# 64, 128 and 32 bytes of gap between the SBUF pools of a two-layer decoder trunk

## The chip, the cores and the metric

The kernel runs on one core of a Trainium2 chip, as one launch. The metric is the device time of that launch in microseconds (us); several runs are taken, and their median counts. The change moves data within SBUF, the core's on-chip memory: 128 partitions, in each of which a tile occupies one range of byte addresses.

## The reference

The program is a decoder trunk of two layers over a sequence of T = 1024 tokens with D = 1024 features, all in float32.

```python
for i in range(2):
    shift_t, scale_t, gate_t, shift_c, scale_c, gate_c = split(silu(c) @ ada_w[i] + ada_b[i], 6)
    h = rmsnorm(x, norm_g[i, 0]) * (1 + scale_t) + shift_t
    y = gla_mixer(h) if i == 0 else diff_mixer(h)
    x = x + gate_t * y
    h = rmsnorm(x, norm_g[i, 1]) * (1 + scale_c) + shift_c
    y = square(relu(h @ mlp_w1[i])) @ mlp_w2[i]          # 1024 -> 4096 -> 1024
    x = x + gate_c * y
return rmsnorm(x, final_g)
```

`gla_mixer` is gated linear attention with 4 heads (keys of 128, values of 256 features), `diff_mixer` differential softmax attention with 8 heads. Both begin with a projection of `h` and end with one of their output (`w_o`).

## The kernel before, in words

**Numbers in two parts.** TensorE gets every large product as three matmuls. `split` (L111) writes a float32 tile as a rounded part (`hi`, by ScalarE) and a remainder (`lo`, by VectorE, here DVE); `mm3` (L115) multiplies hi by hi, hi by lo and lo by hi into one accumulator. So the lines L116, L117 and L118 are the three matmuls of every product, and each group of the profile with these lines stands three times. A matmul has a loaded operand (`lhsT`, 128 x 128, brought into the array by a weight load that the profile shows as PEld) and a streaming one (`rhs`, up to 512 columns). The weight load for the next matmul runs while the present one streams.

**The stages.** Layer 0: the prologue, the GLA projections and their chunked recurrence (`pv`, `pq`, `pk`, then `pr` for the output gate), then `stretch` (L724): output projection, norm, MLP. Layer 1: the attention with its projections `pp` woven between scores and values by a schedule written out by hand, then `stretch` again, and the final norm. The MLP goes through 8 chunks of 512 inner features: for each, 2 halves of 512 tokens times 4 tiles of inner activations `hd` (8 products over `h` each), then 2 halves times 8 output tiles (4 products over `hd` each), which makes 192 matmuls over `h` and 192 over `hd`. In the last chunk the second half of the tokens is taken in two slices of 256 columns. Products go to the accumulators `acc`, `pr`, `pq`, `pk`, `pp`, `pv`; the residual add (L712, DVE) empties the MLP's second product.

**Which operand is which.** In `acc`, `pr`, `pq` and `pk` the weight (`whi`, `wlo`) is loaded and `h` or `hd` streams. In `pp` and `pv` it is the other way round: `h_hi`, `h_lo` are loaded, and `whi`, `wlo` stream, 384 or 256 columns wide (272 in head 0, where 16 more columns of the weight come along).

**Where the tiles lie.** SBUF pools are stacked in the order in which they are opened, and each buffer is rounded up to 32 bytes a partition. `const` comes first, then `wsp` (L89: 5 buffers each of `whi` and `wlo`, 4352 bytes = 17 x 256), `wraw` (L90: 2 x 4352), and `hp` (L91: `h`, 32 buffers of 2048). All three sizes are multiples of 256, so `h` and the weights begin at the same place modulo 256, and as the matmuls take slices at multiples of 512 bytes, each pair of operands does too. The one exception is GLA's head 0: its value weights are `[P, 4, 272]`, whose rows are 1088 = 4 x 256 + 64 bytes apart, so that successive `k` of four begin at 0, 64, 128 and 192 modulo 256 above the weights' base.

In `stretch` four pools follow: `sm` (small columns), `tp` (5 x 2048), `xp` (the residual `x`, tiles of 2048) and `hid` (`hd`, 16 x 2048). Layer 0 opens them in the order sm, tp, xp, hid (L726). `sm` has three small tiles of two buffers there, 6 x 32 = 192 bytes, so `hd` lies 192 bytes above the weights modulo 256. Layer 1 opens xp, hid, tp, sm (L727), and `hd` lies at 0. Two pools of layer 1's attention (`dx`, and `xa1` for half of `x`) are allocated from the other end of SBUF.

Of the kernel before, what the change touches and what calls it, by code (L numbers as in the profile page):

```python
# [10 lines left out]
F32 = mybir.dt.float32  # L11
# [10 lines left out]
P = 128  # L22
# [60 lines left out]
def trunk(ctx: ExitStack, tc, a, out):  # L83
    nc = tc.nc
    pe, act, dve, pool = nc.tensor, nc.scalar, nc.vector, nc.gpsimd
# [2 lines left out]
    const = ctx.enter_context(tc.tile_pool(name="const", bufs=1))  # L88
    wsp = ctx.enter_context(tc.tile_pool(name="wsp", bufs=5))  # L89
    wraw = ctx.enter_context(tc.tile_pool(name="wraw", bufs=2))  # L90
    hp = ctx.enter_context(tc.tile_pool(name="hp", bufs=2 * KT))  # L91
    dram = ctx.enter_context(tc.tile_pool(name="dram", bufs=1, space=DRAM))
    mm = ctx.enter_context(tc.tile_pool(name="mm", bufs=2, space=PSUM))
# [41 lines left out]
    def wcols(w, c0, n, pinned=False):  # L135

        return weight(w.rearrange("(k p) n -> p k n", p=P)[:, :, c0:c0 + n], [P, KT, n], pinned)
# [5 lines left out]
    def new_half():  # L143
        return [(hp.tile([P, HT], F32R, name="h_hi", tag="hhi"), hp.tile([P, HT], F32R, name="h_lo", tag="hlo"))
                for _ in range(KT)]
# [80 lines left out]
    def gscale(l, j):  # L226

        sc = mod[:, l, (3 * j + 1) * KT:(3 * j + 2) * KT]
        i = NG_ROW + (2 * l + j) * KT
        dve.scalar_tensor_tensor(out=gs[:, 2 * l + j, :], in0=sc, scalar=1.0, in1=colsT[:, i:i + KT],  # L230
                                 op0=ALU.add, op1=ALU.mult)

    def mcols(l, i):
        return mod[:, l, i * KT:(i + 1) * KT]
# [445 lines left out]
    def out_proj(h, half, w_o, acc, done, ahead=False, ready=None):  # L680


        rows, ends = KT - 1 if ahead else KT, []
        ws = [wcols(w_o, n * P, P) for n in range(4)]
        if ahead:
            yield
        for n0 in (0, 4):
            now, ws = ws, []
            for n in range(4):
                pt = acc()  # L690
                for k in range(rows):
                    mm3(pt, now[n][0][:, k, :], now[n][1][:, k, :], *h[k][half], k == 0, k == rows - 1)
                    if k == rows - 1:
                        ends.append((n0 + n, half, pt))
                    while ends and (ready is None or ready()):
                        i = done(*ends.pop(0))
                        if n0 == 0:
                            with tc.issue_after(i.ins):
                                ws.append(wcols(w_o, (4 + len(ws)) * P, P))
                    yield  # L700
        if ahead:
            w = weight(w_o.rearrange("(k p) n -> p k n", p=P)[:, rows:, :], [P, 1, D])
            for n in range(KT):
                pt = acc()
                mm3(pt, w[0][:, 0, n * P:(n + 1) * P], w[1][:, 0, n * P:(n + 1) * P], *h[rows][half], True, True)
                done(n, half, pt)
                yield

    def residual(l, x):
        def add(kt, half, psum, cols=slice(0, HT), gate=2):  # L710
            t = x[kt][half][:, cols]
            return dve.scalar_tensor_tensor(out=t, in0=psum, scalar=mcols(l, gate)[:, kt:kt + 1], in1=t, op0=ALU.mult,  # L712
                                            op1=ALU.add)
        return add

    def load_x(x, xp, halves, queue=nc.sync):
        for half in reversed(halves):
            for k in range(KT):
                x[k][half] = xp.tile([P, HT], F32, name=f"x{k}_{half}")
        for half in halves:  # L720
            for k in range(KT):
                queue.dma_start(out=x[k][half], in_=xs[k, :, half * HT:(half + 1) * HT])

    def stretch(l, h, w_o, ada_todo, after, x=None):  # L724
        with ExitStack() as g:
            order = (("sm", 2), ("tp", 5), ("xp", 1), ("hid", 4))  # L726
            order = order if l == 0 else (order[2], order[3], order[1], order[0])  # L727
            pools = {n: g.enter_context(tc.tile_pool(name=n, bufs=b, reuse_waits="tile")) for n, b in order}
            sm, tp, xp, hid = (pools[n] for n in ("sm", "tp", "xp", "hid"))
            ps = g.enter_context(tc.tile_pool(name="lp", bufs=1, space=PSUM, reuse_waits="tile"))  # L730
            ps2 = g.enter_context(tc.tile_pool(name="lp2", bufs=4, space=PSUM, reuse_waits="tile"))
            ga = g.enter_context(tc.tile_pool(name="ga2", bufs=2, reuse_waits="tile")) if ada_todo else None
            turn = [0]

            def acc_tile():
                turn[0] += 1
                shared = turn[0] % 3 == 0
                return (mm if shared else ps2).tile([P, HT], F32, name="acc", tag="mm" if shared else "mx")

            started = x is not None  # L740
            x = x or [[None, None] for _ in range(KT)]
            gscale(l, 1)
            load_x(x, xp, [half for half in range(2) if x[0][half] is None], nc.sync)
            add = residual(l, x)
            h2 = [[None, None] for _ in range(KT)]
            for half in range(2):
                if half or not started:
                    for _ in out_proj(h, half, w_o, acc_tile if half else acc_mm, add):
                        pass
                for k, t in enumerate(new_half()):  # L750
                    h2[k][half] = t
                norm_mod(x, half, h2, gs[:, 2 * l + 1, :], mcols(l, 3), tp, sm, ps)
            h = h2

            w1, w2 = a["mlp_w1"][l], a["mlp_w2"][l]
            sums = []
            for c in range(FF // 512):
                ws = [wcols(w1, c * 512 + n * P, P) for n in range(4)]
                hd = [[None, None] for _ in range(4)]
                for half in range(2):  # L760
                    for n in range(4):
                        pt = acc_tile()
                        for k in range(KT):
                            pe_last = mm3(pt, ws[n][0][:, k, :], ws[n][1][:, k, :], *h[k][half], k == 0, k == KT - 1)
                        if half and n < len(sums):
                            with tc.issue_after(pe_last.ins):
                                ada_sums(*sums[n], ps)
                        r = tp.tile([P, HT], F32, name="relu", tag="t")
                        act.activation(out=r, in_=pt, func=AF.Relu)  # L769
                        dve.tensor_tensor(out=r, in0=r, in1=r, op=ALU.mult)  # L770
                        hd[n][half] = [hid.tile([P, HT], F32R, name="hd", tag=f"hd{half}{i}") for i in range(2)]
                        split(hd[n][half][0], hd[n][half][1], r)
                ws = [weight(w2.rearrange("(f p) n -> p f n", p=P)[:, 4 * c:4 * c + 4, n * 256:(n + 1) * 256],
                             [P, 4, 256]) for n in range(4)]
                last = c == FF // 512 - 1
                for half, cols in ((0, slice(0, HT)), (1, slice(0, 256)), (1, slice(256, HT))) if last else \
                        ((0, slice(0, HT)), (1, slice(0, HT))):
                    w = cols.stop - cols.start
                    finish = after(half, cols, x, tp, sm, ps, acc_tile) if last else None
                    for n in range(KT):  # L780
                        pt = acc_tile()[:, :w]
                        wh, wl = ws[n // 2]
                        c0 = (n % 2) * P
                        for f in range(4):
                            mm3(pt, wh[:, f, c0:c0 + P], wl[:, f, c0:c0 + P], *(t[:, cols] for t in hd[f][half]),
                                f == 0, f == 3)
                        add(n, half, pt, cols, 5)
                        if last and n == 4:
                            next(finish)
                    for _ in finish or ():  # L790
                        pass
                sums = [(*todo, 512, ada_products(*todo, 512, ga, ga, pool, 2)) for todo in ada_todo[:2]]
                del ada_todo[:2]
                assert not (c >= FF // 512 - 2 and ada_todo)
# [394 lines left out]
```

## Time and profile before

| | us |
|---|---|
| median of 3 runs | 2532.35 |
| lowest and highest | 2531.57, 2532.77 |
| the profiled execution's own time | 2536.81 |
| its span in the trace | 2534.9 |

The span goes from the first to the last instruction of the profiled execution; the little around it is launch. A profiled execution has one trace, and all rows below come from it. A timeline row gives the start of an instruction and the time until its result has landed. Matmuls overlap: one begins well before the result of the one ahead has landed, so in a dense stream the time that a matmul costs is the distance between two starts, not its duration. PEclk is the share of full clock granted to TensorE.

### The profile page before, as it was taken

The page shows a single profiled execution, that of the slowest core. Times are in us where ns is not written, and L with a number is a line of the kernel's source. Part 1 is how long each engine was busy: PE and PEld are TensorE (multiplying, and loading weights), DVE is VectorE, ACT ScalarE, POOL GpSimd, SP SyncE. Part 2 cuts the span into 40 slices and gives each one's busy share as a digit, 9 for nine tenths or more (in the row PEclk, how much of TensorE's full clock was granted, in tenths as well). Part 3 has the DMA queues.
Part 4 walks back from the last instruction along what each step waited for, and adds up shares of the span by engine and source line. Part 5 has one row for each costly group of instructions (what it writes and reads, how often), then busy time and mean ns, then how long its engine had stood idle before and what let it go on. Part 6 is the DMA issues. An engine that isn't in the chain of part 4 may idle for free.

```text
span 2534.9 us, 32430 instructions
## 1 busy us (share of the span) xinstructions
PE 2464.6 (97%) x12551; PEld 2112.8 (83%) x12551; DVE 1478.5 (58%) x2872; ACT 914.5 (36%) x1849; POOL 202.3 (8%) x354
## 2 busy tenths in 40 slices
PE   6899999999999999999999999989999999999998
PEld 5788878888888888888999999978788888888887
DVE  7777786654454355334788877887743343334334
ACT  5655555322122122213555555564422112212222
POOL 3011120000010011000221111120000000000000
PEclk8999999999999999999999999999999999999999
DMA  8333374312333243111211111143211111211111
GB/s 286 121 111 117 108 227 129 108 34 68 99 108 98 61 125 96 48 53 61 80 33 35 34 34 34 31 137 102 75 49 52 42 59 34 67 34 58 42 42 67
DMA packets 224026, 202.60 MB, mean 80 GB/s; under 512 B 10426, under 2 KB 194912, under 8 KB 223872
## 3 DMA queue, kind: packets, MB, share of 16 engines
q1 hardware_dynamic: 209472, 156.33, 20.0%
q0 software_dynamic: 12992, 41.97, 5.3%
q8 instruction: 98, 1.61, 0.3%
q10 hardware_dynamic: 1408, 2.24, 0.2%
q14 instruction: 56, 0.46, 0.1%
HBM read 180.57 MB, written 19.92 MB: 79 GB/s over the span
## 4 chain that ended last, share of the span: by engine, by line
PE 44%; DVE 3%; ACT 2%; DMA 2%; issue 1%; DVEq 0%; POOL 0%; ACTq 0%; SPq 0%; POOLq 0%
PE acc L116 10%; PE acc L117 9%; PE acc L118 9%; PE pp L116 3%; PE pp L118 3%; PE pp L117 3%; PE at L967 1%; DMA raw<-in_diff_w_o 1%; PE po L117 1%; PE po L118 1%; PE bc L162 1%; PE po L116 1%; ACT et L937 1%; PE tr L881 0%; PE st L998 0%
## 5 line engine op out<-in xcount | busy, mean ns | idle before, releaser
L116 PE MATMUL acc<-h_hi,whi 128*128 128x512 f32 x1280 | 502.4, 393 | 2.4 <-DVE x L712 2.3
L117 PE MATMUL acc<-h_lo,whi 128*128 128x512 f32 x1280 | 500.0, 391 | 0.0
L118 PE MATMUL acc<-h_hi,wlo 128*128 128x512 f32 x1280 | 500.0, 391 | 0.0
L112 ACT CAST whi<-raw 128x1024 fp32r<-128x1024 f32 (+2 forms) x217 | 221.2, 1020 | 711.8 <-PE acc L117 657.4
L712 DVE SCALAR_TENSOR_TENSOR x<-acc,mod,x 128x512 f32<-128x512 f32 (+1 forms) x312 | 224.3, 723 | 362.2 <-PE acc L118 361.5
L116 PE MATMUL acc<-hd,whi 128*128 128x512 f32 (+1 forms) x1088 | 412.5, 379 | 1.4 <-DVE x L712 1.3
L118 PE MATMUL acc<-hd,wlo 128*128 128x512 f32 (+1 forms) x1088 | 412.3, 379 | 0.0
L117 PE MATMUL acc<-hd,whi 128*128 128x512 f32 (+1 forms) x1088 | 411.9, 379 | 0.0
L113 DVE TENSOR_TENSOR wlo<-raw,whi 128x1024 fp32r<-128x1024 f32 (+2 forms) x217 | 258.4, 1191 | 136.2 <-ACT whi L112 129.0
L116 PEld LDWEIGHTS acc<-h_hi,whi 128*128 128x128 f32 x1280 | 240.9, 188 | 52.0 <-DVE x L712 3.4
L118 PEld LDWEIGHTS acc<-h_hi,wlo 128*128 128x128 f32 x1280 | 241.0, 188 | 50.5
L117 PEld LDWEIGHTS acc<-h_lo,whi 128*128 128x128 f32 x1280 | 241.1, 188 | 48.6
L116 PEld LDWEIGHTS acc<-hd,whi 128*128 128x128 f32 x1088 | 204.2, 188 | 42.7 <-DVE x L712 1.8
L118 PEld LDWEIGHTS acc<-hd,wlo 128*128 128x128 f32 x1088 | 204.3, 188 | 40.9
L117 PEld LDWEIGHTS acc<-hd,whi 128*128 128x128 f32 x1088 | 204.1, 188 | 40.9
L770 DVE TENSOR_TENSOR relu<-relu 128x512 f32<-128x512 f32 x128 | 88.0, 688 | 205.8 <-ACT relu L769 205.8
L116 PE MATMUL pp<-whi,h_hi 128*128 128x384 f32 x512 | 182.8, 357 | 0.0
L118 PE MATMUL pp<-whi,h_lo 128*128 128x384 f32 x512 | 172.7, 337 | 0.0
L117 PE MATMUL pp<-wlo,h_hi 128*128 128x384 f32 x512 | 172.3, 336 | 0.3 <-DVE nm L934 0.3
L207 POOL DMA_DIRECT2D ada_raw<-in_ada_w x160 | 85.9, 537 | 867.4 <-DVE ada_acc L210 529.4
L769 ACT ACTIVATE relu<-acc 128x512 f32<-128x512 f32 x128 | 75.8, 593 | 219.5 <-PE acc L118 219.5
L112 ACT CAST hd<-relu 128x512 fp32r<-128x512 f32 x128 | 79.5, 621 | 164.4 <-DVE relu L770 164.3
(1761 smaller groups left out, 3817.3 us busy)
## 6 DMA issues: line engine op xcount, KB each, us to landing
raw<-in_mlp_w SPq DMA_DIRECT2D x128, 512.0 KB, 3.6
ada_raw<-in_ada_w POOLq DMA_DIRECT2D x160, 256.0 KB, 3.4
raw<-in_gla_w_in SPq DMA_DIRECT2D x24, 512.0 KB, 4.3
raw<-in_diff_w_in SPq DMA_DIRECT2D x64, 192.0 KB, 2.9
raw<-in_diff_w_o SPq DMA_DIRECT2D x17, 512.0 KB, 4.0
aw<-in_ada_w SPq DMA_DIRECT2D x16, 512.0 KB, 7.6
raw<-in_gla_w_o SPq DMA_DIRECT2D x16, 512.0 KB, 4.0
x<-xs SPq DMA_DIRECT2D x32, 256.0 KB, 5.5
```

Of the source, the lines that this page charges most:

```text
L112: act.copy(out=hi, in_=src)
L113: dve.tensor_tensor(out=lo, in0=src, in1=hi.bitcast(F32), op=ALU.subtract)
L116: pe.matmul(out=o, lhsT=lh, rhs=rh, start=start, stop=False)
L117: pe.matmul(out=o, lhsT=lh, rhs=rl, start=False, stop=False)
L118: return pe.matmul(out=o, lhsT=ll, rhs=rh, start=False, stop=stop)
L162: pe.matmul(out=bc[:, j * P:(j + 1) * P], lhsT=cols[:, j:j + 1].broadcast_to([P, P]), rhs=ident, start=True, stop=True)
L207: queue.dma_start(out=w, in_=a["ada_w"][l].rearrange("(k p) n -> p k n", p=P)[:, k:k + kk, c0:c0 + n])
L712: return dve.scalar_tensor_tensor(out=t, in0=psum, scalar=mcols(l, gate)[:, kt:kt + 1], in1=t, op0=ALU.mult, op1=ALU.add)
L769: act.activation(out=r, in_=pt, func=AF.Relu)
L770: dve.tensor_tensor(out=r, in0=r, in1=r, op=ALU.mult)
L937: act.activation(out=et[:, n * HT:n * HT + wn], in_=p[:, :wn], func=AF.Exp, bias=nm, scale=DH ** -0.5, accum_out=ssum[:, s, n:n + 1])
L967: pe.transpose(out=at[:, n * P:(n + 1) * P], in_=pair["es"][i][:, j * P:(j + 1) * P], identity=ident)
```

## The change

One tile of 16 float32 (64 bytes a partition) is put between `wraw` and `hp`, and one of 32 (128 bytes, layer 0) or 56 (224 bytes, layer 1) at the beginning of `xp`. Each is written once by DVE and never read.

```diff
     wraw = ctx.enter_context(tc.tile_pool(name="wraw", bufs=2))
+    gap = ctx.enter_context(tc.tile_pool(name="gap", bufs=1))
+    dve_gap = gap.tile([P, 16], F32, name="gap_h")
+    dve.memset(dve_gap, 0.0)
     hp = ctx.enter_context(tc.tile_pool(name="hp", bufs=2 * KT))
...
             sm, tp, xp, hid = (pools[n] for n in ("sm", "tp", "xp", "hid"))
+            dve.memset(xp.tile([P, 32 if l == 0 else 56], F32, name="gap"), 0.0)
             ps = g.enter_context(tc.tile_pool(name="lp", bufs=1, space=PSUM, reuse_waits="tile"))
```

Modulo 256 and above the weights, `h` goes from 0 to 64. `hd` of layer 0 goes from 192 to 64 + 192 + 128 = 384, which is 128; `hd` of layer 1 from 0 to 64 + 224 = 288, which is 32. The weights stay where they were. Every other pool of the lower end moves up by 64 bytes (in a stretch, what lies above the gap by as much more), so that pairs of tiles among them keep their distances.

## Rows read from the trace of the kernel before

**Rows 1.** The page: its span, and TensorE's busy time, share and instructions.
```profile
span 2534.9 us, 32430 instructions
PE 2464.6 (97%) x12551; PEld 2112.8 (83%) x12551; DVE 1478.5 (58%) x2872; ACT 914.5 (36%) x1849; POOL 202.3 (8%) x354
```
**Rows 2.** Groups by form, TensorE, whole span: count, busy us, mean ns, idle before.
```profile
L116 PE MATMUL acc<-h_hi,whi 128*128 128x512 f32 x1280 | 502.4, 393 | 2.4 <-DVE x L712 2.3
...
L116 PE MATMUL acc<-hd,whi 128*128 128x512 f32 x960 | 375.9, 392 | 0.0
...
L116 PE MATMUL pp<-whi,h_hi 128*128 128x384 f32 x512 | 182.8, 357 | 0.0
...
L116 PE MATMUL pv<-whi,h_hi 128*128 128x256 f32 x192 | 57.4, 299 | 3.3 <-DVE vt L113 1.8 <-DVE t L462 1.4
...
L116 PE MATMUL pr<-h_hi,whi 128*128 128x512 f32 x128 | 50.5, 395 | 0.0
...
L116 PE MATMUL acc<-hd,whi 128*128 128x256 f32 x128 | 36.6, 286 | 1.4 <-DVE x L712 1.3
```
**Rows 3.** Timeline, TensorE, layer 0's first chunk: start us, duration us, instruction.
```profile
547.25 0.39 PE L116 MATMUL acc<-hd,whi 128*128 128x512 f32 x1
...
592.05 0.39 PE L116 MATMUL acc<-h_hi,whi 128*128 128x512 f32 x1
...
593.20 0.39 PE L118 MATMUL acc<-h_hi,wlo 128*128 128x512 f32 x1
```
**Rows 4.** Timeline, TensorE, a chunk of layer 1.
```profile
1863.53 0.39 PE L116 MATMUL acc<-hd,whi 128*128 128x512 f32 x1
...
1907.05 0.39 PE L116 MATMUL acc<-h_hi,whi 128*128 128x512 f32 x1
...
1950.57 0.39 PE L116 MATMUL acc<-hd,whi 128*128 128x512 f32 x1
```
**Rows 5.** Timeline, TensorE, projections of layer 1: first of six, and the next after them.
```profile
1651.32 0.33 PE L116 MATMUL pp<-whi,h_hi 128*128 128x384 f32 x1
...
1652.36 0.39 PE L922 MATMUL ps__15831<-k,qh 128*128 128x512 f32 x1
```
**Rows 6.** Timeline, TensorE, the last chunk's 256-column slices, layers 0 and 1.
```profile
1202.03 0.28 PE L117 MATMUL acc<-hd,whi 128*128 128x256 f32 x1
...
1204.38 0.28 PE L116 MATMUL acc<-hd,whi 128*128 128x256 f32 x1
...
2512.69 0.28 PE L116 MATMUL acc<-hd,whi 128*128 128x256 f32 x1
...
2514.49 0.28 PE L116 MATMUL acc<-hd,whi 128*128 128x256 f32 x1
```
**Rows 7.** Timeline, TensorE, GLA's first unit, head 0: k = 5, 6 and 7.
```profile
55.37 0.29 PE L116 MATMUL pv<-whi,h_hi 128*128 128x272 f32 x1
...
56.89 0.39 PE L116 MATMUL pq<-h_hi,whi 128*128 128x512 f32 x1
...
60.23 0.28 PE L116 MATMUL pv<-whi,h_hi 128*128 128x272 f32 x1
...
61.49 0.40 PE L116 MATMUL pq<-h_hi,whi 128*128 128x512 f32 x1
...
62.88 0.29 PE L116 MATMUL pv<-whi,h_hi 128*128 128x272 f32 x1
...
64.36 0.39 PE L116 MATMUL pq<-h_hi,whi 128*128 128x512 f32 x1
```
**Rows 8.** Windows: stretch, its us, busy us of each engine, PEclk, DMA share, GB/s.
```profile
547.20:592.00 44.80, 44.80 (x193) 35.91 (x193) 17.37 (x21) 5.33 (x6) 0.00 (x0) 1.00 0.16 49
...
1221.00:1680.00 459.00, 447.81 (x2855) 430.85 (x2854) 367.93 (x1092) 262.99 (x724) 87.18 (x154) 1.00 0.14 41
```

## The prediction

> **What bounds the kernel now.** I read the page first: TensorE is busy for 2464.6 of 2534.9 us, 97% [rows 1]. No other engine comes near, so what the change is worth must come out of TensorE's own work, and waits are a side matter. The by-form groups say where that work is [rows 2]: each row is one of the three matmuls of `mm3`, so a group counts three times. Matmuls that stream 512 columns of `h` past a weight are 3 x 1280 (`acc`) and 3 x 128 (`pr`), 4224 together; those that stream the MLP's inner activations `hd` are 3 x 960, 1440 in each layer, and 3 x 128 more of 256 columns. In the projections of layer 1 (`pp`, 3 x 512) and of the GLA values (`pv`, 3 x 192) the roles are exchanged: `h` is the loaded operand, the weight streams.
>
> The means in those groups overlap each other, so they are no price. The price is the distance from one start to the next, which I call the step. In layer 0 a chunk's 192 `hd` matmuls start at 547.25 us and the next group at 592.05 [rows 3]: 44.80 / 192 = 233.3 ns. In layer 1 the same 192 take 1863.53 to 1907.05, 43.52 / 192 = 226.7 ns, and the 192 `h` matmuls behind them again 43.52 us [rows 4]. The clock granted is 1.00 in these stretches, the 2.4 GHz level [rows 8], at which 512 columns take 213.3 ns. So 13.3 ns are lost in one place and 20.0 in the other, two and three times 6.67 ns, which is 16 columns or 64 bytes a partition. Shapes, types, helper line and weights' pool are the same; what differs is where `hd` lies: 192 bytes above the weights modulo 256 in layer 0, 0 bytes in layer 1. The placement therefore has a price, and it comes in slots of 6.67 ns per matmul.
>
> [...]
>
> **The change part by part.** Relative to the weights, `h` goes from 0 to 64, `hd` of layer 0 from 192 to 128, `hd` of layer 1 from 0 to 32. I need the step at each new place.
>
> *`hd` of layer 0, 192 to 128.* No 512-column row stands at 128. The nearest are those of the first GLA unit, whose head-0 weight rows are 1088 bytes apart, so that successive `k` stream at 64, 128 and 192 above the loaded `h`, 272 columns each (113.3 ns of columns) [rows 7]. At 64: 12 matmuls from 55.37 to 56.89, 126.7 ns, 13.3 lost. At 128: 10 from 60.23 to 61.49, 126.0, 12.7 lost. At 192: 12 from 62.88 to 64.36, 123.3, 10.0 lost. So 64 and 128 look like 0 (two slots) and only 192 is odd. I take 226.7 ns at 128: 1440 x 6.67 ns = **-9.6 us**. Bounds: 0 if it stays at 233.3, -19.2 us if it falls by two slots to 220.0. The 256-column part steps at 117.5 ns in layer 0 (1202.03 to 1204.38, 20 matmuls) and at 120.0 in layer 1 (2512.69 to 2514.49, 15) [rows 6]; about half of the 384 lie in each layer, and 192 x 2.5 ns = **+0.5 us**.
>
> *`h`, 0 to 64, 4224 matmuls.* By the row at 64 [rows 7] I take no change, **0**. Bounds: one slot either way, 28.2 us. That row is not conclusive: at 192 the short matmuls lose less than at 0 (10.0 ns here, 10.8 at 256 columns [rows 6]) while the 512-column ones lose more, so width can turn the order round.
>
> *`hd` of layer 1, 0 to 32, 1440 matmuls.* No row has a 32-byte distance; all distances in the long streams are multiples of 64. Between its neighbours 0 and 64, both at two slots, I take **0**; bounds -9.6 and +9.6 us.
>
> *`pp` and `pv`.* With `h` moved up by 64, the streaming weight now lies 64 below it, 192 modulo 256: the bad place of layer 0. `pp` has 384 columns (160 ns) and steps at 173.3 ns (1651.32 to 1652.36, six) [rows 5]. At 192 the 256-column rows gain 2.5 ns, the 512-column rows pay 6.67. Half way lies 2.1 ns, and I take it, since 384 is half way too: 1536 x 2.1 = **+3.2 us**; bounds -3.8 and +10.2. TensorE is busy for 447.81 of 459.00 us there [rows 8], so nothing covers it. `pv` has 256 columns in heads 1 to 3: 576 x -2.5 = **-1.4 us**, at worst 0. In head 0 the four distances only change places.
>
> *The rest.* Three memsets of at most 56 columns come onto DVE, one at the start and one at each stretch. DVE is busy for 17.37 us of 44.80 in an MLP chunk [rows 8], so they cost nothing. A memset waits for the old tile under its address; behind it in DVE's queue stand the gate columns and the residual adds, which free the accumulators, so a long wait would reach TensorE two tiles later. The tile under it in layer 1 is a query tile that the last head leaves long before its end; in layer 0 one of the decay gate. No DMA and no queue is moved.
>
> **Sum:** -9.6 + 0.5 + 0 + 0 + 3.2 - 1.4 = -7.3 us. The profiled execution took 2536.81 us, 4.46 above the median of 2532.35; the sum makes it 2529.5, and the median **2525.1 us**.
>
> **Rivals.**
>
> *A: each new place loses a slot fewer than 0 does, because any distance except 0 and 192 keeps the two readers apart.* Then 4224 + 1440 matmuls fall from 226.7 to 220.0 and 1440 from 233.3 to 220.0: 28.2 + 9.6 + 19.2 = 57.0 us; with +3.2 and -1.4 it is 2477.1 us. For it: the loss differs with the place at all, and 13.3 ns are left to win. Against it: the rows at 64 and 128 [rows 7], whose loss is that of 0.
>
> [...]
>
> *B: `h` at 64 falls into the third slot.* The step of the `h` matmuls becomes 233.3 as in layer 0's `hd`, +28.2 us, and 2525.1 + 28.2 = 2553.3 us: slower. It decides as soon as more than a quarter of the 4224 pay the slot (7.3 of 28.2 us). For it: after layer 0's `hd` stretch the first five `h` matmuls take 592.05 to 593.20, 230 ns each, before the stream settles [rows 3]; a place at which it never settles would stay there or above. Against it: the row at 64.
>
> *C: the distance is not what sets the step.* Something else that differs between the layers' `hd` streams, such as which banks the products go to, would leave 2532 us. For it: one pair of stretches alone shows the effect. Against it: `h` in both layers steps alike, and the 256-column rows differ too.
>
> [...]
>
> **How the numbers follow.** Forecast and its neighbourhood 0.40, A 0.30, B 0.18, C 0.12. A measurement of this kernel can tell some 0.2% (5 us) from no change. Within the forecast the `pp` term decides: without it 10.5 us are gained, with all 10.2 of it nothing; I give 0.28 to a gain over 5 us and 0.12 to less. So faster 0.28 + 0.30 = 0.58, same 0.12 + 0.12 = 0.24, slower 0.18. Low end: A with `pp` at its lower bound, 2477.1 - 7.0 = 2470. High end: the forecast with `pp` at +10.2 (7.0 more) and layer 1's `hd` a slot up (9.6), 2525.1 + 16.6 = 2542. B alone is left out.
>
> **What would show it.** Right: layer 0's `hd` chunk takes 43.5 us instead of 44.8, layer 1's `hd` and the `h` chunks stay at 43.5, `pp` steps between 171 and 180 ns. Wrong: `h` chunks near 42.2 us (A) or 44.8 (B), or layer 0's `hd` chunk still 44.8 (C).

## The result, and the profile after

The changed kernel takes 2553.01 us (median of 4 runs, 2551.37 to 2556.16) against 2532.56 for the kernel before: a ratio of 1.0082, with a 95% interval of 1.0065 to 1.0100. It is slower, by some 20 us, where 7 us less was forecast.

The page and the groups by form of the kernel after, TensorE; the three helper lines are now L119, L120 and L121, three lines further down.

```profile
span 2549.7 us, 32432 instructions
PE 2478.5 (97%) x12551; PEld 2112.1 (83%) x12551; DVE 1477.2 (58%) x2875; ACT 915.0 (36%) x1849; POOL 201.6 (8%) x354
```
```profile
L119 PE MATMUL acc<-h_hi,whi 128*128 128x512 f32 x1280 | 503.3, 393 | 2.5 <-DVE x L715 2.4
...
L119 PE MATMUL acc<-hd,whi 128*128 128x512 f32 x960 | 379.1, 395 | 0.0
...
L119 PE MATMUL pp<-whi,h_hi 128*128 128x384 f32 x512 | 182.8, 357 | 0.0
...
L119 PE MATMUL pv<-whi,h_hi 128*128 128x256 f32 x192 | 57.9, 302 | 4.1 <-DVE t L465 2.1 <-DVE vt L116 1.9
```

Against [rows 1, 2] TensorE has the same 12551 instructions and the same share. Of the 14.8 us by which the two spans differ, 13.9 are its busy time. Waits have hardly grown: in front of `acc<-h_hi` it sat idle for 2.5 us instead of 2.4, in front of `pv` for 4.1 instead of 3.3. Among the means, that of `hd` has grown (395 ns instead of 392) and that of `pp` has not (357). But the durations of matmuls overlap, so the chunks have to be read by their starts. The timeline of the kernel after, TensorE: the first `hd` chunk of layer 0 and what follows it; then in layer 1 an `hd` chunk, the `h` chunk behind it and what follows that.

```profile
551.92 0.39 PE L119 MATMUL acc<-hd,whi 128*128 128x512 f32 x1
...
596.53 0.39 PE L119 MATMUL acc<-h_hi,whi 128*128 128x512 f32 x1
```
```profile
1866.11 0.40 PE L119 MATMUL acc<-hd,whi 128*128 128x512 f32 x1
...
1910.91 0.40 PE L119 MATMUL acc<-h_hi,whi 128*128 128x512 f32 x1
...
1954.87 0.40 PE L119 MATMUL acc<-hd,whi 128*128 128x512 f32 x1
```

192 matmuls each, to be held against [rows 3, 4]:

| stream | distance before, after | us for 192, before | after | step in ns, before | after |
|---|---|---|---|---|---|
| `hd`, layer 0 | 192, 128 | 44.80 | 44.61 | 233.3 | 232.3 |
| `hd`, layer 1 | 0, 32 | 43.52 | 44.80 | 226.7 | 233.3 |
| `h` | 0, 64 | 43.52 | 43.96 | 226.7 | 229.0 |

Here and below, distance means how far the streaming tile lies above the loaded one modulo 256 bytes.

The step of `h` is also of another kind than before. In the kernel before three steps make 0.68 us (from this line of its timeline to 1950.57 in [rows 4]) and are alike, 226 or 227 ns each:

```profile
1949.89 0.39 PE L116 MATMUL acc<-h_hi,whi 128*128 128x512 f32 x1
```

After the change the single steps differ from each other (timeline of the kernel after, within that `h` chunk):

```profile
1930.84 0.39 PE L119 MATMUL acc<-h_hi,whi 128*128 128x512 f32 x1
1931.07 0.39 PE L120 MATMUL acc<-h_lo,whi 128*128 128x512 f32 x1
1931.30 0.39 PE L121 MATMUL acc<-h_hi,wlo 128*128 128x512 f32 x1
1931.53 0.39 PE L119 MATMUL acc<-h_hi,whi 128*128 128x512 f32 x1
1931.75 0.39 PE L120 MATMUL acc<-h_lo,whi 128*128 128x512 f32 x1
1931.98 0.39 PE L121 MATMUL acc<-h_hi,wlo 128*128 128x512 f32 x1
```

Three steps make 0.69 us here (1930.84 to 1931.53). A timeline rounds to 10 ns; by the starts in whole ns that the trace holds, the three steps are 226, 229 and 232 ns, over and over. The clock was granted in full, as before (windows of the kernel after: stretch, its us, busy us of each engine, PEclk, DMA share, GB/s); VectorE is as little busy as in [rows 8].

```profile
551.92:596.53 44.61, 44.61 (x194) 36.17 (x192) 17.36 (x21) 5.28 (x6) 0.00 (x0) 1.00 0.16 48
...
1866.11:1910.91 44.80, 44.80 (x193) 35.99 (x192) 17.35 (x21) 5.29 (x6) 0.00 (x0) 1.00 0.16 48
1910.91:1954.87 43.96, 43.96 (x193) 36.06 (x192) 15.08 (x19) 12.46 (x19) 0.00 (x0) 1.00 0.16 48
```

### The profile page after: what moved, and what is told of

Its sections match the earlier page's. It is cut to its first block, busy times and chain, and to the rows that moved or that the text cites. A ratio compares the mean times of both kernels' runs of the same rounds, so it can differ in the third digit from the quotient of the medians.

```text
span 2549.7 us, 32432 instructions
## 1 busy us (share of the span) xinstructions
PE 2478.5 (97%) x12551; PEld 2112.1 (83%) x12551; DVE 1477.2 (58%) x2875; ACT 915.0 (36%) x1849; POOL 201.6 (8%) x354
## 4 chain that ended last, share of the span: by engine, by line
PE 45%; DVE 2%; ACT 2%; DMA 1%; issue 1%; DVEq 0%; POOL 0%; ACTq 0%; SPq 0%; POOLq 0%
PE acc L120 10%; PE acc L121 10%; PE acc L119 10%; PE pp L119 3%; PE pp L121 3%; PE pp L120 3%; PE at L971 1%; DMA raw<-in_diff_w_o 1%; ACT et L941 1%; PE po L120 1%; PE po L121 1%; PE bc L165 1%; PE po L119 1%; PE tr L885 0%; PE st L1002 0%
## 5 line engine op out<-in xcount | busy, mean ns | idle before, releaser
L119 PE MATMUL acc<-h_hi,whi 128*128 128x512 f32 x1280 | 503.3, 393 | 2.5 <-DVE x L715 2.4
L121 PE MATMUL acc<-h_hi,wlo 128*128 128x512 f32 x1280 | 503.2, 393 | 0.0
L120 PE MATMUL acc<-h_lo,whi 128*128 128x512 f32 x1280 | 503.1, 393 | 0.0
L119 PE MATMUL acc<-hd,whi 128*128 128x512 f32 (+1 forms) x1088 | 415.6, 382 | 1.3 <-DVE x L715 1.2
L121 PE MATMUL acc<-hd,wlo 128*128 128x512 f32 (+1 forms) x1088 | 415.3, 382 | 0.0
L120 PE MATMUL acc<-hd,whi 128*128 128x512 f32 (+1 forms) x1088 | 415.0, 381 | 0.0
L116 DVE TENSOR_TENSOR wlo<-raw,whi 128x1024 fp32r<-128x1024 f32 (+2 forms) x217 | 258.4, 1191 | 136.2 <-ACT whi L115 127.8
L119 PEld LDWEIGHTS acc<-h_hi,whi 128*128 128x128 f32 x1280 | 240.8, 188 | 55.2 <-DVE x L715 3.5
L120 PEld LDWEIGHTS acc<-h_lo,whi 128*128 128x128 f32 x1280 | 241.1, 188 | 51.6
L121 PEld LDWEIGHTS acc<-h_hi,wlo 128*128 128x128 f32 x1280 | 241.1, 188 | 51.2
L119 PEld LDWEIGHTS acc<-hd,whi 128*128 128x128 f32 x1088 | 204.5, 188 | 44.7 <-DVE x L715 1.7
L121 PEld LDWEIGHTS acc<-hd,wlo 128*128 128x128 f32 x1088 | 204.5, 188 | 43.2
L120 PEld LDWEIGHTS acc<-hd,whi 128*128 128x128 f32 x1088 | 204.5, 188 | 43.0
L119 PE MATMUL pp<-whi,h_hi 128*128 128x384 f32 x512 | 182.8, 357 | 0.0
L121 PE MATMUL pp<-whi,h_lo 128*128 128x384 f32 x512 | 172.4, 337 | 0.0
L120 PE MATMUL pp<-wlo,h_hi 128*128 128x384 f32 x512 | 172.3, 337 | 0.0
```

The costliest lines, as they stand in the source:

```text
L116: dve.tensor_tensor(out=lo, in0=src, in1=hi.bitcast(F32), op=ALU.subtract)
L119: pe.matmul(out=o, lhsT=lh, rhs=rh, start=start, stop=False)
L120: pe.matmul(out=o, lhsT=lh, rhs=rl, start=False, stop=False)
L121: return pe.matmul(out=o, lhsT=ll, rhs=rh, start=False, stop=stop)
```

## The experiments

**Theory D**: a 512-column matmul's step is set by the distance of its streaming tile from the loaded one modulo 256, and by nothing else that the change touches. Its rivals: that the moves of `h` and `hd` need each other (E), that the layer or operand counts and not the place (L), that the place itself counts and not the distance (F). The first four experiments take the change apart; their ratios are to runs of the kernel before on the same chip, whose median there was 2534.84 us.

**One: only `h` moves.** The gap before `hp` stays, and the stretches' gaps put `hd` back at 192 and 0. The edit is against the kernel after.

```diff
-            dve.memset(xp.tile([P, 32 if l == 0 else 56], F32, name="gap"), 0.0)
+            dve.memset(xp.tile([P, 48 if l == 0 else 48], F32, name="gap"), 0.0)
```

> Only h moves: 64 bytes above the weights modulo 256; the stretches' gaps are 192 bytes each, so that hd stays at 192 (layer 0) and 0 (layer 1). Theory D (the step of a 512-column matmul is set by the distance of its streaming tile from the loaded one modulo 256: 226.7 ns at 0, 228.9 at 64, 232.4 at 128, 233.3 at 192, 233.3 at 32): the 192 h matmuls of an MLP chunk take 43.9 us instead of 43.5, hd stays at 44.8 and 43.5 us; 4608 matmuls by 2.2 ns make +10 us, 2542 us. Rival E (the two moves need each other: what is seen in hd comes from h's unsettled stream ahead of it): hd of layer 1 is at 44.8 us here too, and the time near 2550 us.

Measured 2541.9 us (6 runs), ratio 1.0030 (1.0017 to 1.0042). Timeline of this kernel, layer 1: an `hd` chunk, the `h` chunk behind it, and what follows.

```profile
1863.44 0.39 PE L119 MATMUL acc<-hd,whi 128*128 128x512 f32 x1
...
1906.99 0.40 PE L119 MATMUL acc<-h_hi,whi 128*128 128x512 f32 x1
...
1950.95 0.40 PE L119 MATMUL acc<-hd,whi 128*128 128x512 f32 x1
```

`hd` 43.55 us, `h` 43.96 us: `h` pays with `hd` at rest, and `hd` of layer 1 is left alone, so E falls for these two.

**Two: only `hd` moves.** No gap before `hp`; the stretches' gaps are 48 and 8 elements, which puts `hd` at 128 and 32. From here on the edits are against the kernel before.

```diff
+            dve.memset(xp.tile([P, 48 if l == 0 else 8], F32, name="gap"), 0.0)
```

> Only hd moves: 128 (layer 0) and 32 (layer 1) above the weights, by gaps of 192 and 32 bytes; h stays at 0. Theory D: an hd chunk takes 44.6 us in layer 0 (44.8 before) and 44.8 us in layer 1 (43.5 before), h chunks 43.5 us; -1.3 + 9.6 = +8.3 us, 2541 us. Rival E: hd of layer 1 stays at 43.5 us and the time at 2532 us.

Measured 2542.95 us (5 runs), ratio 1.0034 (1.0021 to 1.0048). Timeline of this kernel, the same places:

```profile
1860.92 0.40 PE L116 MATMUL acc<-hd,whi 128*128 128x512 f32 x1
...
1905.73 0.40 PE L116 MATMUL acc<-h_hi,whi 128*128 128x512 f32 x1
...
1949.29 0.40 PE L116 MATMUL acc<-hd,whi 128*128 128x512 f32 x1
```

`hd` 44.81 us, `h` 43.56 us: as D has it. Layer 0 is a miss. Its first `hd` chunk, at 128:

```profile
547.27 0.40 PE L116 MATMUL acc<-hd,whi 128*128 128x512 f32 x1
...
592.07 0.39 PE L116 MATMUL acc<-h_hi,whi 128*128 128x512 f32 x1
```

That is 44.8 us and not the 44.6 that the kernel after shows. With `h` at 0, `hd` is no better at 128 than at 192; the 1.0 ns a matmul that the kernel after gains at 128 goes with where `h` lies. So something of E is left in layer 0, and D's "nothing else" does not hold at 128. The two halves nearly add up: 1.0030 and 1.0034 make 1.0064, just below the whole change's interval (1.0065 to 1.0100), and each half is uncertain by 0.0012 or more itself.

**Three: only layer 0's `hd` moves, to 0** (and with it the residual `x`, whose pool lies between the gap and `hd`).

```diff
+            if l == 0:
+                dve.memset(xp.tile([P, 16], F32, name="gap"), 0.0)
```

> Only layer 0's hd moves, from 192 to 0, by a gap of 64 bytes; everything else as before. Theory D: an hd chunk of layer 0 takes 43.5 us, as in layer 1, 1440 x 6.67 ns = -9.6 us, 2523 us. Rival L (the step belongs to the layer, not to the place): it stays at 44.8 us and 2532 us.

Measured 2526.26 us (5 runs, 2522.67 to 2528.55), ratio 0.9961 (0.9947 to 0.9976): faster than both kernels. Timeline of this kernel, layer 0's first `hd` chunk:

```profile
550.77 0.39 PE L116 MATMUL acc<-hd,whi 128*128 128x512 f32 x1
...
594.29 0.39 PE L116 MATMUL acc<-h_hi,whi 128*128 128x512 f32 x1
```

43.52 us, to the hundredth what layer 1 needs. L falls: the same matmuls in the same layer get 6.67 ns shorter each by 64 bytes of placement. That `x` moves too is settled by experiments nine to eleven, which leave `x` of layer 0 where it lies here and move `hd` alone: its steps change again.

**Four: everything above `const` moves up by 64 bytes.** The gap stands ahead of the weights' pool, so that the distances stay 0, 192 and 0.

```diff
+    gap = ctx.enter_context(tc.tile_pool(name="gap", bufs=1))
+    dve_gap = gap.tile([P, 16], F32, name="gap_h")
+    dve.memset(dve_gap, 0.0)
     wsp = ctx.enter_context(tc.tile_pool(name="wsp", bufs=5))
```

> A gap of 64 bytes ahead of the weights' pool: weights, h and hd all move up together and keep their distances 0, 192 and 0. Theory D: steps and time as before, 2532 us, within 3 us. Rival F (the place itself counts, not the distance): steps of h change from 226.7 ns, and the time by up to 10 us either way.

Measured 2534.56 us (10 runs), ratio 1.0001 (0.9991 to 1.0010). Timeline of this kernel, the chunks of [rows 3, 4]:

```profile
547.11 0.39 PE L119 MATMUL acc<-hd,whi 128*128 128x512 f32 x1
...
591.91 0.39 PE L119 MATMUL acc<-h_hi,whi 128*128 128x512 f32 x1
...
1860.56 0.39 PE L119 MATMUL acc<-hd,whi 128*128 128x512 f32 x1
...
1904.08 0.39 PE L119 MATMUL acc<-h_hi,whi 128*128 128x512 f32 x1
...
1947.60 0.39 PE L119 MATMUL acc<-hd,whi 128*128 128x512 f32 x1
```

The chunks take 44.80 (`hd`, layer 0), 43.52 (`hd`, layer 1) and 43.52 us (`h`, layer 1), as before. For a shift by 64 bytes F falls, and with it the thought that the memset at the start or the shifted addresses of other pools cost something.

**Five to eight: a map of distances.** One run each, `h` at 0, `hd` of the two layers at different places by the elements of the stretches' gaps:

```diff
+            dve.memset(xp.tile([P, A if l == 0 else B], F32, name="gap"), 0.0)
```

with A, B = 32, 32 (distances 64 and 128), 24, 48 (32 and 192), 40, 56 (96 and 224), 56, 16 (160 and 64).

> A map of distances, h at 0: hd of layer 0 at 64, of layer 1 at 128, by gaps of 128 bytes each. Theory D: an hd chunk of layer 0 steps like h at 64, 228.9 ns (43.9 us), one of layer 1 like layer 0's hd at 128, 232.4 ns (44.6 us). Rival L (step set by the operand or the layer): other values, 233.3 and 226.7 ns.

> Map: hd of layer 0 at 32, of layer 1 at 192, by gaps of 96 and 192 bytes. Theory D: both 233.3 ns (44.8 us a chunk), since 233.3 was seen at 32 in layer 1 and at 192 in layer 0. Rival L: layer 0 keeps 233.3, layer 1 has 226.7 at 192.

> Map: hd of layer 0 at 96, of layer 1 at 224, by gaps of 160 and 224 bytes. New distances. Theory D with slots: between 226.7 and 233.3 ns at both. Rival G (some distance has no loss at all, and the change only missed it): 213.3 to 220 ns at one of them.

> Map: hd of layer 0 at 160, of layer 1 at 64, by gaps of 224 and 64 bytes. Theory D: layer 1 at 228.9 ns as h at 64; layer 0 between 226.7 and 240. Rival G: 213.3 to 220 ns at 160.

**Nine and ten: a finer map.** `hd` is cut out of tiles that are 256 bytes longer, at an offset of 16 and 8 bytes, then 240 and 248; layer 0's pool is first brought to 0 as in experiment three.

```diff
-                        hd[n][half] = [hid.tile([P, HT], F32R, name="hd", tag=f"hd{half}{i}") for i in range(2)]
+                        at = (4, 4) if l == 0 else (2, 2)
+                        hd[n][half] = [hid.tile([P, HT + 64], F32R, name="hd", tag=f"hd{half}{i}")[:, at[i]:at[i] + HT]
+                                       for i in range(2)]
```

> A finer map, h at 0: hd of layer 0 at 16 bytes above the weights modulo 256, of layer 1 at 8, cut out of tiles 256 bytes longer. Theory S (0 is a single place at which the streams settle, every other one costs 229 to 234 ns): steps between 229 and 234 ns in both layers. Rival Z (the good place is a zone around 0): 226.7 ns in both. Rival G (somewhere the loss is smaller): 213.3 to 220 ns.

> The other side of 0: hd of layer 0 at 240, of layer 1 at 248 bytes above the weights modulo 256. Theory S: 229 to 234 ns in both layers. Rival Z: 226.7 ns in both. Rival G: 213.3 to 220 ns.

What was measured of `hd`, 192 matmuls of 512 columns, first chunk of the layer that was read (start of the first to start of the next group); in the kernels before and after the other chunks of a layer repeat it to 0.02 us (44.61 to 44.63 in layer 0 after). `h` lies at 0 except in the two rows of the kernel after:

| distance | kernel and layer | us for 192 | step, ns |
|---|---|---|---|
| 0 | before, layer 1; three, layer 0 | 43.52; 43.52 | 226.7 |
| 8 | nine, layer 1 | 44.81 | 233.4 |
| 16 | nine, layer 0 | 44.47 | 231.6 |
| 32 | two, layer 1; six, layer 0 | 44.81; 44.80 | 233.4 |
| 32 | after, layer 1 (`h` at 64) | 44.80 | 233.3 |
| 64 | five, layer 0; eight, layer 1 | 43.96; 43.97 | 229.0 |
| 96 | seven, layer 0 | 44.82 | 233.4 |
| 128 | two, layer 0; five, layer 1 | 44.80; 44.79 | 233.3 |
| 128 | after, layer 0 (`h` at 64) | 44.61 | 232.3 |
| 160 | eight, layer 0 | 44.98 | 234.3 |
| 192 | before, layer 0; six, layer 1 | 44.80; 44.80 | 233.3 |
| 224 | seven, layer 1 | 44.80 | 233.3 |
| 240 | ten, layer 0 | 44.80 | 233.3 |
| 248 | ten, layer 1 | 44.80 | 233.3 |

The rows of nine (both layers) and of ten (layer 0), timelines of these kernels:

```profile
547.02 0.39 PE L116 MATMUL acc<-hd,whi 128*128 128x512 f32 x1
...
591.49 0.39 PE L116 MATMUL acc<-h_hi,whi 128*128 128x512 f32 x1
...
1853.93 0.40 PE L116 MATMUL acc<-hd,whi 128*128 128x512 f32 x1
...
1898.74 0.39 PE L116 MATMUL acc<-h_hi,whi 128*128 128x512 f32 x1
```
```profile
549.93 0.40 PE L116 MATMUL acc<-hd,whi 128*128 128x512 f32 x1
...
594.73 0.39 PE L116 MATMUL acc<-h_hi,whi 128*128 128x512 f32 x1
```

Five distances (0, 32, 64, 128 and 192) were measured in both layers with `h` at 0; each gives the same step in either. So neither the layer nor another pool sets it, but the distance does, with the one exception that at 128 the place of `h` counts for 1.0 ns. 0 is the best of the twelve, and it is a single place: 8 bytes above or below it the whole 6.67 ns are back. No distance came down to 220 ns, so the rival with a smaller loss (G) falls at all places that were tried. Five is a miss at 128: 232.4 ns were expected and 233.3 measured, as in two. The times are 2537.14, 2544.70, 2545.39 and 2538.25 us for five to eight, beside 2531.76 for the kernel before on that chip, and 2537.55 and 2545.24 for nine and ten, beside 2536.54. Single runs of one kernel lie up to 9 us apart (2530.82 to 2540.17 in experiment four), so the steps say more than these.

**Eleven: hi and lo apart.** As in nine, with `at` = (0, 16) in layer 0 and (16, 0) in layer 1, in elements: one part of `hd` at 0, the other at 64 bytes.

> Layer 0: the hi part of hd at 0, the lo part at 64; layer 1: hi at 64, lo at 0. The second of the three matmuls streams lo, the two others hi. If each matmul's step is set by its own pair alone: 226.7, 229.0, 226.7 ns in layer 0 (43.67 us for 192) and 229.0, 226.7, 229.0 in layer 1 (43.82 us). Rival M (a matmul's step depends on the state that those ahead of it left): lines whose pair lies at 0 leave 226.7 ns too, and the mean of three can be over 229 ns.

Measured 44.54 us in layer 0 and 44.80 in layer 1 (2543.21 us in all): far from 43.67 and 43.82, the sums of single prices. Timeline of this kernel, three triples of layer 0; L116 and L118 stream hi, whose distance is 0:

```profile
570.36 0.39 PE L116 MATMUL acc<-hd,whi 128*128 128x512 f32 x1
570.59 0.40 PE L117 MATMUL acc<-hd,whi 128*128 128x512 f32 x1
570.82 0.40 PE L118 MATMUL acc<-hd,wlo 128*128 128x512 f32 x1
571.07 0.39 PE L116 MATMUL acc<-hd,whi 128*128 128x512 f32 x1
571.29 0.39 PE L117 MATMUL acc<-hd,whi 128*128 128x512 f32 x1
571.51 0.39 PE L118 MATMUL acc<-hd,wlo 128*128 128x512 f32 x1
571.74 0.40 PE L116 MATMUL acc<-hd,whi 128*128 128x512 f32 x1
```

From 570.82 to 571.07 the L118 matmul takes 0.25 us, from 571.51 to 571.74 0.23: the same pair, another step. So a matmul's step is not set by its own pair alone, as D has it; rival M, by which those ahead of it count, is left. In neither mixture did the stream settle at 226.7 ns.

## Why the prediction was wrong

**The main reading held.** TensorE's steps carry the change, no wait or other engine does; distances have a price; [rows 3, 4] priced 0 and 192 rightly: in experiment three 192 matmuls go from 44.80 to 43.52 us by 64 bytes of distance. Rival C, that the distance does nothing, falls with it. The 213.3 ns from which the prediction counts losses is an estimate that its rows at distance 0 bear out: 256 columns step at 120.0 ns [rows 6], 384 at 173.3 [rows 5] and 512 at 226.7 [rows 4], which is 53.3 ns for each 128 columns, or 2.4 columns a ns (the prediction writes 2.4 GHz) at a granted clock of 1.00. By that slope 512 columns take 213.3 ns, and 13.3 ns are left over at each of the three widths. Whether it is the weight load that takes them is not shown, since no run streams without one.

**The step that failed** is the one that priced 512-column streams by the 272-column rows: "So 64 and 128 look like 0 (two slots) and only 192 is odd." For 512 columns it is the other way round: 0 is odd, 64 costs 2.3 ns more, and 128 costs what 192 does, within 1.0 ns. Nor does the price come "in slots of 6.67 ns": 16 costs 4.9 ns and 160 7.6. Three terms hang on it.

- *`hd` of layer 0 at 128*, forecast -9.6 us. Measured 232.3 ns beside 233.3, 1440 x -1.0 = -1.4 us, and by experiment two nothing at all when `h` rests.
- *`h` at 64*, forecast 0, with one slot either way as bounds. Measured 2.3 ns (43.96 against 43.52 us), a third of a slot: 4224 x 2.3 = +9.7 us. Experiment one, timed by itself, gives 0.30% or +7.6 us. (The 4224 leave out `pq` and `pk`, 384 more matmuls that stream 512 columns of `h`; at 2.3 ns they would add 0.9 us.)
- *`hd` of layer 1 at 32*, forecast 0 as it lies "Between its neighbours 0 and 64". Measured the upper bound, +6.67 ns, 1440 x 6.67 = +9.6 us. To interpolate between two places was no better than the row that it leant on.

The sum of the three is +17.9 us, within the interval of the whole (0.65 to 1.00% of 2532.56, 16.5 to 25.3 us); what lies between 17.9 and 20.4 is not placed. These 2.5 us are less than the scatter of single runs: the two profiled executions, 2536.81 and 2551.69 us, differ by 14.9 us only.

**The warning stood in the rows.** The prediction saw that 192 loses less than 0 at 256 and 272 columns and more at 512, said that "width can turn the order round", and still took the narrow rows' order for the wide ones. The kernel after shows the turn once more. In the last chunk of layer 1 the 256-column slices of `hd` at 32 step at 116.7 ns (timeline of the kernel after, 15 matmuls, 2528.04 to 2529.79, 1.75 us), better than the 120.0 at 0 in [rows 6], while its 512-column chunks at 32 are worse than at 0.

```profile
2528.04 0.28 PE L119 MATMUL acc<-hd,whi 128*128 128x256 f32 x1
...
2529.79 0.28 PE L119 MATMUL acc<-hd,whi 128*128 128x256 f32 x1
```

And at 256 columns a place does not even have one price. The 117.5 ns at 192 that the prediction read in [rows 6] is one of two values: 8 us earlier in the same trace the same slices, at the same distance, step at 113.3 ns (timeline of the kernel before, 18 matmuls, 2.04 us).

```profile
1194.38 0.28 PE L116 MATMUL acc<-hd,whi 128*128 128x256 f32 x1
...
1196.42 0.28 PE L116 MATMUL acc<-hd,whi 128*128 128x256 f32 x1
```

**Small terms.** `pp` at 192 was priced at +3.2 us and cost nothing: in a steady stretch it steps at 173.3 ns as in [rows 5] (timeline of the kernel after, 24 matmuls, 4.16 us), and from its first start to its last 456.3 us pass (1227.1 to 1683.4), where it was 458.6 (1221.2 to 1679.8).

```profile
1229.29 0.34 PE L119 MATMUL pp<-whi,h_hi 128*128 128x384 f32 x1
...
1233.45 0.34 PE L119 MATMUL pp<-whi,h_hi 128*128 128x384 f32 x1
```

`pv` was to gain 1.4 us. Its step does fall as forecast in a steady stretch, from 120.0 ns (kernel before, 24 matmuls from 286.52 to 289.40) to 117.5 (kernel after, 24 from the first to the second of these lines).

```profile
289.64 0.28 PE L119 MATMUL pv<-whi,h_hi 128*128 128x256 f32 x1
...
292.46 0.28 PE L119 MATMUL pv<-whi,h_hi 128*128 128x256 f32 x1
```

But from the first `pv` to the last, waits and other work included, 268.3 us pass after (29.1 to 297.4) and 265.4 before (29.0 to 294.4), and 263.7 in experiment one (29.2 to 292.9), where `pv` lies as it does after. A gain of 1.4 us can't be told in that. The memsets cost nothing, as said: experiment four has the one at the start and the time of before, and experiment three has one in layer 0's stretch and gains 0.39%, 9.9 us, where its matmuls gain 9.6.

**The rivals.** B gave 2553.3 us, and the measured time is 2553.0, but that is no success of its mechanism: it had `h` pay a whole slot, and `h` pays a third; the rest comes from layer 1's `hd`, which no rival had. Of A nothing is left: no 512-column stream lost a slot less, and its two readers were the author's guess, which no run shows. The range missed at its top, 2542 us, since each of these terms was bounded by itself and the top took only two of them, `pp` and layer 1's `hd`, together. It left out `h` at any price ("B alone is left out", though B had 0.18) and the bound at which layer 0's `hd` gains nothing.

**What stays open** is why. The runs show that the steps at 64 go 226, 229, 232 ns over and over, and that one pair in experiment eleven takes 0.25 us and then 0.23, but not what makes them do so. `h` at places other than 0 and 64 was not tried, nor `hd` at distances finer than 8 bytes.

## What to carry to other kernels

In a dense stream of 512-column float32 products measure the distance between starts, not the mean duration, and compare streams of one shape that differ only in where their operands lie: 6.67 of 233 ns hung on it here. In streams of 512 columns distance 0 stepped at 226.7 ns and the eleven other distances at 229.0 to 234.3, so where such tiles begin at the same place modulo 256 bytes, leave them there, and see to it that small tiles opened in between don't push a pool off; a gap of 64 bytes that brought layer 0's `hd` back to 0 was worth 0.39%. A price by place was good only for the column count at which it was read: 192 cost 6.67 ns more than 0 at 512 columns and 2.5 less at 256 in [rows 6]. A short stretch can show one of several: the 256-column slices at 192 stepped at 117.5 and at 113.3 ns in one trace.

## What was not expected of the hardware

The good place is a single one. Of twelve distances 0 alone lets 512-column streams settle at 226.7 ns; 8 and 248 bytes, its nearest neighbours, have 233.4 and 233.3. At 256 columns the order differs: 120.0 ns at 0, 117.5 or 113.3 at 192, 116.7 at 32. Streams off the good place settled into rhythms of unequal steps: by the starts in the trace, 226, 229 and 232 ns at 64, and 229 and 238 by turns at 128 (experiment five, layer 1). And a settled stream repeats itself: all seven `hd` chunks of 192 matmuls of 512 columns take the same time to 0.02 us, 44.80 us in layer 0 and 43.52 in layer 1 before, 44.61 to 44.63 and 44.79 to 44.80 after.
